# Attention scores as two products over 128 rows, with another order of the attention steps

## The chip, the cores and the metric

The kernel runs on one core of one Trainium2 chip. The engines of a core work side by side, each through its own queue in order: TensorE (PE, with its weight loads shown as PEld), VectorE (DVE), ScalarE (ACT), GpSimd (POOL), and SyncE (SP), which issues the DMAs. The metric is the device time of one run in microseconds; the lower the better.

## What is computed

The reference is one inference step of two trunk layers over 640 tokens of width 1024: 128 context tokens and 512 latent ones. A layer is an FFN, a mixer of four head groups (A, B, C, D), and a second FFN. The change lies in mixers A and B, which are attention with four query heads of width 64 over two key/value heads:

```python
q = rms_norm(q.reshape(B, T, n_kv, n_q // n_kv, HEAD_DIM), gq)
k = rms_norm(k.reshape(B, T, n_kv, HEAD_DIM), gk)
...
# B, dense, 128-query blocks; latent tokens read 256 cached and 512 own keys
s = jnp.einsum('bqkgd,bskd->bkgqs', qi, k).astype(jnp.float32) * scale
p = attn_probs(s, sink).astype(v.dtype)
return jnp.einsum('bkgqs,bskd->bqkgd', p, v)
...
# A, windowed: 256 cached keys and a band of up to 384 own keys, with a sink
s_band = jnp.einsum('bnqkgd,bnskd->bnkgqs', qb, kb).astype(jnp.float32) * scale
s_band = jnp.where(valid[None, :, None, None], s_band, NEG_INF)
s_ctx = jnp.einsum('bnqkgd,bckd->bnkgqc', qb, kc).astype(jnp.float32) * scale
```

Everything is float32. A context block (128 queries) reads only its own 128 keys.

## The kernel before

A float32 operand of a product is kept as two parts of a faster type (fp32r): `hi`, a rounded copy, and `lo`, the rest. A product of two such operands is three matmuls, hi·hi, hi·lo and lo·hi (`mm3`, lines 271 to 275, tiles `...h` and `...l`).

The mixer of a layer (`mixers`, from line 840 on) is written as Python generators, one for each strand of work, and each letter of the string `ORDER` (lines 40 to 42) runs one of them to its next `yield`: C and L the convolution and scan of mixer C, a, b, v, r, s mixer D, p and q the projections of A's and of B's queries, keys and values (`qkv`, a first step that takes the weights and five blocks of 128 tokens, twice), t and u their transposes (`qktr`), m and n the scores and softmax of A and of B, M and N the transposes of the probabilities and the products with the values behind them, c one half of an output chunk of the product of mixers C and D with the output weights (`down`, written `dn`), and "!" the load of the cached keys and values. At "|" PSUM is cut anew into two score tiles of two banks (`psS`) and four tiles of one bank (`psM`), which the projections (`nat`), transposes (`tr`, `pt`), products with values (`ao`) and `dn` share. A scheduler then sets the final order on each engine from this sequence, so neighbouring steps may be interleaved.

One step m or n is one head of one block of 128 queries, called a head here; there are 20 for A and 20 for B in each layer. Four of the 20 are the context block (128 keys), and the other 16 are long: 768 keys in B, 512 or 640 in A. TensorE makes its scores (`sc`) with the queries as the stationary operand. The head's 64 dimensions lie on 64 of the 128 partitions, the lower half for key/value head 0 and the upper for 1:

```python
r = slice(kv * 64, kv * 64 + 64)
qh, ql = qkh[g][r, b * 128:b * 128 + 128], qkl[g][r, b * 128:b * 128 + 128]
...
mm3(p[:, 256:512], qh, ql, ckh[r, ...], ckl[r, ...], True, True)
mm3(p[:, 512:512 + w], qh, ql, qkh[2][r, k0:k0 + w], qkl[2][r, k0:k0 + w], True, not band)
```

A band's edge is masked by one more matmul of 128 columns (line 1257). VectorE finds the maximum (`mx`, line 1264) and its negative (`nm`), ScalarE takes the exponential (`P`, line 1273), VectorE the reciprocal of the sum and the scaling of `P` (lines 1279, 1280). Then TensorE transposes `P` in pieces of 128 (line 1290), ScalarE copies them out (`PT`, 1291), TensorE multiplies with the values (1299), and ScalarE and VectorE split the result into parts (`mxh`, `mxl`, 1303, 1304). In a projection block ScalarE copies and squares (1173, 1174), VectorE and GpSimd normalise and rotate (1178 to 1201); `tr` (1154) transposes queries and keys with the tokens on columns and splits them (1160, 1161).

The weights come through a pool of 15 tiles (`wide`), shared with `P` and `PT`; ScalarE and VectorE split them (lines 168, 169).

Of the kernel before, what the change touches and what calls it, by code (L numbers as in the profile page):

```python
# [4 lines left out]
F32 = mybir.dt.float32  # L5
F32R = mybir.dt.float32r
# [19 lines left out]
HALF = ((320, 640), (0, 320))  # L26
EPS = 1e-6
# [13 lines left out]
    "CaCCCCvLvrLarvvvLLLbsLvpLrprbrssrqsrsrLsptrsLpppqLp|!sputpLsptcqpcmccpMmqMmmcqtMmMmmqmMMmmqMqMcmcqMm"  # L41
    "MuqmmqqccMMMmmmucMmMnnnuNcNNnnNnMNnnMNNmMncNncnnNNcnnNnNmnNNNMnNnNNnMccnMNNN",) * L
# [11 lines left out]
def trunk(tc, A, O):  # L54
# [3 lines left out]
    with ExitStack() as es:  # L58
# [7 lines left out]
        def banks(two, one):  # L66
            """PSUM as `two` tiles of two banks and `one` tiles of one"""
# [8 lines left out]
        def other():  # L76
            """the end of the stack of pools changes its form between the FFNs and the mixers"""
# [40 lines left out]
        # ---------------------------------------------------------------- constants, residual, conditions  # L118
# [18 lines left out]
        # ---------------------------------------------------------------- weights, prefetched in order  # L137
# [21 lines left out]
        def parts(src, n):  # L159
            """the two parts of a float32 operand"""  # L160
# [16 lines left out]
        def take(ahead=2, deep=0):  # L177
            """the next weights; those of the next `ahead` items are made, the next `deep` of them loaded"""
# [15 lines left out]
        def halved(ap, n):  # L194
            """a load of two items"""
# [5 lines left out]
        def seven(gate, up):  # L201
            """the weights of the seven products of one hidden chunk: gate = [A11 | A12], up = [A21 | A22]"""
# [68 lines left out]
        def mm3(out, wh, wl, xh, xl, first, last, more=False):  # L271
            """out (+)= w x, three products of their parts; `more` goes on with sums that were read already"""
# [11 lines left out]
        # ---------------------------------------------------------------- modulation  # L284
        # per (layer, group): tile [128, 2 conditions (latent, context), 8 chunks]
# [24 lines left out]
        def mod_row(l, g, k, c):  # L310
            """one condition's products for 128 columns of w_mod"""
# [19 lines left out]
        def after_start(n=""):  # L331
            """what is not needed at once issues behind the first norm"""
# [6 lines left out]
        def mod_load(k):  # L339
            """w_mod for the first norm's shift and scale, chunk k"""  # L340
# [7 lines left out]
        def mod_first(k):  # L348
            """shift and scale of the first norm, chunk k: eight products in four column groups, then their sum"""
# [49 lines left out]
        # ---------------------------------------------------------------- norm  # L399
# [437 lines left out]
        def mixers(l):  # L837
# [685 lines left out]
```

## Time and profile before

| | us |
|---|---|
| three runs | 2520.03, 2520.49, 2522.44 (median 2520.49) |
| profiled execution, span from its first to its last instruction | 2521.9 |
| first layer, last retention norm of D to the norm after the mixer | 637.1 to 837.0 |
| first score product, first and second layer | 656.8 and 1897 |
| last score product, first and second layer | 803 and 2041 |

The profile is of another execution than the three runs; its own time is known by its span alone, 1.4 us over the median of the runs. TensorE is busy for 98% of the span, VectorE for 78%, ScalarE for 45%. A matmul's shown length runs on past the start of the next, so a busy TensorE is not TensorE at its peak: what one product costs is read from start to start in the timeline. The two layers are alike, and the sections below read the first one.

### The profile page before, as it was taken

How to read it: one execution, taken by the hardware profiler on the slowest of the kernel's cores; microseconds unless marked ns; L12 is line 12 of the kernel's file. 1: busy time of each engine (PE TensorE's matmuls, PEld its weight loads, DVE VectorE, ACT ScalarE, POOL GpSimd, SP SyncE). 2: the span in 40 equal slices, each digit the busy share in tenths (PEclk: the TensorE clock that was granted, in tenths of full speed). 3: DMA queues.
4: the chain of work that ended last, by engine and by line, in shares of the span. 5: the costliest groups of instructions: out<-in, count | busy, mean ns of one | idle time of the engine just before them, and what ended most of it. 6: DMA issues, size and time to landing. Idle time of an engine off the chain costs nothing.

```text
span 2521.9 us, 43865 instructions
## 1 busy us (share of the span) xinstructions
PE 2467.4 (98%) x17376; PEld 2365.6 (94%) x17376; DVE 1974.8 (78%) x3850; ACT 1141.8 (45%) x2271; POOL 244.8 (10%) x251
## 2 busy tenths in 40 slices
PE   7999999999999999999999999999999999999999
PEld 6999999996888999999999999999878789999999
DVE  6899989856666898988989898897656668666765
ACT  5344334563345633443463344344634556433433
POOL 2100000022420200000020000000433102000000
PEclk9999999999999999999999999999999999999999
DMA  7544344222102244443424444342110022222222
GB/s 253 185 152 138 127 129 148 94 78 67 37 18 66 93 144 134 143 133 118 141 89 148 134 142 133 119 134 78 58 60 26 18 76 76 77 67 81 87 81 71
DMA packets 92303, 261.88 MB, mean 104 GB/s; under 512 B 10049, under 2 KB 20929, under 8 KB 92097
## 3 DMA queue, kind: packets, MB, share of 16 engines
q1 hardware_dynamic: 92096, 259.07, 31.7%
q8 instruction: 137, 2.24, 0.4%
q14 instruction: 70, 0.57, 0.1%
HBM read 255.63 MB, written 3.41 MB: 103 GB/s over the span
## 4 chain that ended last, share of the span: by engine, by line
PE 67%; DVE 4%; ACT 2%; POOL 1%; issue 1%; DVEq 0%; POOLq 0%; ACTq 0%
PE dn L273 8%; PE dn L274 7%; PE dn L275 7%; PE x L274 5%; PE x L275 5%; PE x L273 5%; PE y L274 3%; PE y L275 3%; PE y L273 3%; PE pt L1290 2%; PE ao L1299 2%; PE g L274 2%; PE g L273 2%; PE g L275 1%; PE z L273 1%; PE z L274 1%
## 5 line engine op out<-in xcount | busy, mean ns | idle before, releaser
L273 PE MATMUL dn<-hidh,wp 128*128 128x320 f32 x1408 | 434.5, 311 | 0.0
L275 PE MATMUL dn<-hidh,wp 128*128 128x320 f32 x1408 | 433.9, 309 | 0.0
L274 PE MATMUL dn<-hidl,wp 128*128 128x320 f32 x1408 | 433.7, 309 | 0.2 <-DVE hidl L281 0.2
L168 ACT ACTIVATE wp<-ws 128x512 fp32r<-128x512 f32 x288 | 180.8, 630 | 393.2 <-DVE ws L215 149.9
L168 ACT ACTIVATE wp<-raw 128x512 fp32r<-128x512 f32 (+1 forms) x408 | 243.7, 611 | 212.1 <-DVE wp L169 84.2
L682 DVE SCALAR_TENSOR_TENSOR x<-dn,mod,x 128x128 f32<-128x128 f32 (+3 forms) x488 | 233.8, 518 | 126.4 <-PE dn L275 125.3
L318 DVE SCALAR_TENSOR_TENSOR junk<-wm,cond 128x1024 bf16<-128x1024 f32 x256 | 304.5, 1218 | 4.6 <-DMA wm<-in_wmod 4.5
L169 DVE TENSOR_TENSOR wp<-raw,wp 128x512 fp32r<-128x512 f32 (+1 forms) x408 | 266.2, 667 | 51.9 <-ACT wp L168 47.0
L273 PEld LDWEIGHTS dn<-hidh,wp 128*128 128x128 f32 x1408 | 264.5, 188 | 4.8 <-ACT hidh L280 3.7
L274 PEld LDWEIGHTS dn<-hidl,wp 128*128 128x128 f32 x1408 | 264.8, 188 | 0.6 <-DVE hidl L281 0.6
L275 PEld LDWEIGHTS dn<-hidh,wp 128*128 128x128 f32 x1408 | 264.6, 188 | 0.0
L169 DVE TENSOR_TENSOR wp<-ws,wp 128x512 fp32r<-128x512 f32 x288 | 197.4, 691 | 17.6 <-ACT wp L168 17.0
L274 PE MATMUL g<-hl,whi 128*128 128x320 f32 x608 | 192.6, 318 | 3.2 <-DVE hl L528 1.7
L275 PE MATMUL g<-hh,wlo 128*128 128x320 f32 x608 | 190.5, 314 | 0.0
L273 PE MATMUL g<-hh,whi 128*128 128x320 f32 x608 | 185.5, 318 | 4.5 <-ACT hh L527 2.2
L273 PE MATMUL x<-hh,wp 128*128 128x320 f32 x576 | 178.3, 310 | 1.0 <-DVE sl L613 1.0
L274 PE MATMUL x<-hl,wp 128*128 128x320 f32 x576 | 178.5, 310 | 0.0
L275 PE MATMUL x<-hh,wp 128*128 128x320 f32 x576 | 178.3, 309 | 0.0
L169 DVE TENSOR_TENSOR wlo<-raw,whi 128x1024 fp32r<-128x1024 f32 x88 | 109.8, 1249 | 61.2 <-ACT whi L168 46.0
L425 POOL TENSOR_TENSOR nrs<-nrm,neghalf 80x4 f32<-80x4 f32 x12 | 13.3, 1106 | 1377.1 <-DVE nrm L423 1377.1
L168 ACT ACTIVATE whi<-raw 128x1024 fp32r<-128x1024 f32 x88 | 92.5, 1052 | 80.5 <-PE dk L274 20.7
L274 PEld LDWEIGHTS g<-hl,whi 128*128 128x128 f32 x608 | 117.1, 193 | 5.9 <-DVE hl L454 3.5
(331 smaller groups left out, 6655.2 us busy)
## 6 DMA issues: line engine op xcount, KB each, us to landing
raw<-in_wgu SPq DMA_DIRECT2D x176, 512.0 KB, 3.5
wm<-in_wmod SPq DMA_DIRECT2D x128, 512.0 KB, 4.0
raw<-in_wd SPq DMA_DIRECT2D x64, 512.0 KB, 3.8
raw<-in_wd SPq DMA_DIRECT2D x32, 384.0 KB, 3.4
raw<-in_wint SPq DMA_DIRECT2D x20, 512.0 KB, 3.5
wm<-in_wm SPq DMA_DIRECT2D x32, 256.0 KB, 5.5
raw<-in_wqkv SPq DMA_DIRECT2D x16, 512.0 KB, 3.5
raw<-in_wocd SPq DMA_DIRECT2D x8, 512.0 KB, 3.4
```

The lines of the kernel that those rows point to most:

```text
L168: S.activation(hi, src, AF.Copy)
L169: V.tensor_sub(lo, src, hi.bitcast(F32))
L273: PE.matmul(out, wh, xh, start=first, stop=False, skip_group_check=more)
L274: PE.matmul(out, wh, xl, start=False, stop=False, skip_group_check=more)
L275: mark["pe"] = PE.matmul(out, wl, xh, start=False, stop=last, skip_group_check=more)
L318: V.scalar_tensor_tensor(junk, modraw["w"], 1.0, cond[c], OP.mult, OP.mult, accum_out=modraw[(l, g)][:, c, k:k + 1])
L425: G.tensor_tensor(r, s, neghalf[:80, :4], op=OP.pow)
L682: V.scalar_tensor_tensor(x[d][:, s0:s1], pv[:, s0 - base:s1 - base], gate[:, c, d:d + 1], x[d][:, s0:s1], OP.mult, OP.add)
L1290: PE.transpose(p[:, c0 - a0:c0 - a0 + 128], P[:, c0:c0 + 128], idn)
L1299: PE.matmul(o[kv * 64:kv * 64 + 64, :128], vs[i][:, kv * 64:kv * 64 + 64], pts[kv][:, i * 128:i * 128 + 128], start=i == 0, stop=i == nb - 1)
```

## The change

Queries are no longer kept as a hi tile and a lo tile with two key/value heads on the two halves of the partitions. For each key/value head there is one tile `q2` of all 128 partitions: hi on the 64 rows of that head, lo on the other 64. Keys are doubled: a tile `kkh` (hi) and a tile `kkl` (lo) for each key/value head hold the same 64 rows twice. A product of `q2` with `kkh` over 128 rows is hi·hi + lo·hi, and one with `kkl` is hi·lo + lo·lo. So `mm2` makes two matmuls where `mm3` made three. To double the keys, the last addition of the key projection writes them twice (`qq`, 256 columns in place of 128), and the transposes of keys take two pieces in place of one. The copies and splits out of PSUM are made per 64 rows for queries. The cached keys are loaded with two DMAs for each key/value head and split per head, in `wide` tiles. `ORDER` is new after "|": "!" stands behind the projections, right ahead of the first m; eight of the twelve steps q come before the first m (three before); c steps are spread, five before the first n (ten before) and eleven behind. The rest of the diff takes comments out.

```diff
+ROWS = (slice(0, 64), slice(64, 128))
 ORDER = (
-    "...Lp|!sputpLsptcqpcmccpMmqMmmcqtMmMmmqmMMmmqMqMcmcqMm"
-    "MuqmmqqccMMMmmmucMmMnnnuNcNNnnNnMNnnMNNmMncNncnnNNcnnNnNmnNNNMnNnNNnMccnMNNN",) * L
+    "...Lp|spqtpqLsptqpqpqtq!mqmmqMmqMmMmqMmMmuMmcMmuMmMmcM"
+    "mMmuMmcMmuMmMmcMmMmcMnMnMMncNnNncNnNncNnNncNnNncNnNnNncNnNncNnNncNnNnNNcNcNc",) * L
...
                 def tr(tiles, blocks, chunks):
-                    for i_, c in enumerate(chunks):
+                    t0, n = blocks[0] * 128, len(blocks) * 128
+                    c = slice(t0, t0 + n)
+                    if len(chunks) == 1 and not ks:
+                        ks.extend((slot("kkh", F32R, T), slot("kkl", F32R, T)) for _ in ROWS)
+                    if len(chunks) == 2 and not qs:
+                        qs.extend([slot("q2", F32R, T) for _ in ROWS] for _ in range(2))
+                    for i_ in range(2):
                         p = psM("tr")
-                        t0, n = blocks[0] * 128, len(blocks) * 128
                         for i, b in enumerate(blocks):
                             PE.transpose(p[:, i * 128:i * 128 + 128], tiles[b][:, i_ * 128:i_ * 128 + 128], idn)
-                        S.activation(qk[0][c][:, t0:t0 + n], p[:, :n], AF.Copy)
-                        V.tensor_sub(qk[1][c][:, t0:t0 + n], p[:, :n], qk[0][c][:, t0:t0 + n].bitcast(F32))
+                        if len(chunks) == 1:
+                            hi, lo = ks[i_]
+                            S.activation(hi[:, c], p[:, :n], AF.Copy)
+                            V.tensor_sub(lo[:, c], p[:, :n], hi[:, c].bitcast(F32))
+                        else:
+                            for kv in range(2):
+                                t, r, o = qs[i_][kv], ROWS[kv], ROWS[1 - kv]
+                                S.activation(t[r, c], p[r, :n], AF.Copy)
+                                V.tensor_sub(t[o, c], p[r, :n], t[r, c].bitcast(F32))
...
+                        if pas == 0:
+                            twice = thin("qq", 256)
...
+                            if b == 0:
+                                S.activation(out, q4, AF.Copy)
+                            else:
+                                V.tensor_add(out, q4, r4)
+                            q = twice
...
             def load_cache():
-                ck = slot("ck", F32, 512)
-                D.dma_start(out=ck, in_=A["ck"][l])
+                cache["k"] = []
+                for kv in range(2):
+                    ck = wide("ck", 512)
+                    for r in ROWS:
+                        D.dma_start(out=ck[r], in_=A["ck"][l][ROWS[kv]])
+                    cache["k"].append(parts(ck, 512))
...
                 def scores(b, g, kv):
-                    r = slice(kv * 64, kv * 64 + 64)
-                    qh, ql = qkh[g][r, b * 128:b * 128 + 128], qkl[g][r, b * 128:b * 128 + 128]
+                    q2 = qs[g][kv][:, b * 128:b * 128 + 128]
+
+                    def mm2(out, keys, c, last=True):
+                        PE.matmul(out, q2, keys[0][:, c], start=True, stop=False)
+                        PE.matmul(out, q2, keys[1][:, c], start=False, stop=last)
...
-                        mm3(p[:, 256:512], qh, ql, ckh[r, m * 256:m * 256 + 256], ckl[r, m * 256:m * 256 + 256], True, True)
+                        mm2(p[:, 256:512], cache["k"][kv], slice(m * 256, m * 256 + 256))
...
-                        mm3(p[:, 512:512 + w], qh, ql, qkh[2][r, k0:k0 + w], qkl[2][r, k0:k0 + w], True, not band)
+                        mm2(p[:, 512:512 + w], ks[kv], slice(k0, k0 + w), not band)
```

Three places in the built order show what moves, all in the first layer. Line numbers of the changed kernel differ from those of the kernel before.

On TensorE, a head of B with the transposes around it, before:

```order
L1290 MATMUL pt<-idn,P 128x128 x3
L273 MATMUL sc<-ckh,qkh 128x256
L274 MATMUL sc<-ckl,qkh 128x256
L275 MATMUL sc<-ckh,qkl 128x256
L273 MATMUL sc<-qkh 128x512
L274 MATMUL sc<-qkl,qkh 128x512
L275 MATMUL sc<-qkh,qkl 128x512
L1290 MATMUL pt<-idn,P 128x128 x9
```

and now (the cached keys' parts are called `wp`):

```order
L1323 MATMUL pt<-idn,P 128x128 x6
L1271 MATMUL sc<-wp,q_8001 128x256
L1272 MATMUL sc<-wp,q_8001 128x256
L1271 MATMUL sc<-kkh,q_8001 128x512
L1272 MATMUL sc<-kkl,q_8001 128x512
L1323 MATMUL pt<-idn,P 128x128 x6
L1332 MATMUL ao<-PT,cv 64x128 x4
```

Six score products have become four, and each pair of `ao` products over both heads stands between heads as it did.

On VectorE, among the long heads of A, before (`q`, `r`, `qss` are the projection blocks of step q):

```order
L1178 TENSOR_REDUCE qss<-qsq 128x4
L1179 TENSOR_SCALAR qss<-qss 128x4
L1183 TENSOR_TENSOR q<-q,qrr 128x256
L1277 TENSOR_TENSOR sum<-sum,esink 128x1
L1197 TENSOR_TENSOR r<-q,rsin 128x8x16 x2
L1279 RECIPROCAL rc<-sum 128x1
L1280 TENSOR_SCALAR P<-P,rc 128x640
L1201 TENSOR_TENSOR q<-q,r 128x256
L1161 TENSOR_TENSOR qkl<-tr,qkh 128x512
L1264 TENSOR_REDUCE mx<-sc 128x1
L1178 TENSOR_REDUCE qss<-qsq 128x4
L1268 TENSOR_SCALAR nm<-mx,negsink 128x1
```

and now:

```order
L1313 TENSOR_SCALAR P<-P,rc 128x640
L1337 TENSOR_TENSOR mxl<-ao,mxh 128x128
L1297 TENSOR_REDUCE mx<-sc 128x1
L1301 TENSOR_SCALAR nm<-mx,negsink 128x1
L1169 TENSOR_TENSOR kkl<-tr,kkh 128x512 x2
L1297 TENSOR_REDUCE mx<-sc 128x1
L170 TENSOR_TENSOR wlo<-raw,whi 128x1024
L1301 TENSOR_SCALAR nm<-mx,negsink 128x1
L170 TENSOR_TENSOR wlo<-raw,whi 128x1024
L1310 TENSOR_TENSOR sum<-sum,esink 128x1
L1312 RECIPROCAL rc<-sum 128x1
L1313 TENSOR_SCALAR P<-P,rc 128x640
```

The projection blocks have gone from between the heads (they stand ahead of the first head); the splits of doubled keys of B and of output weights stand there now.

On ScalarE, the split of the cached keys (`ckh` before, `wp<-ck` now), before:

```order
L168 ACTIVATE whi<-raw 128x1024
L1119 ACTIVATE so<-st 64x256
L280 ACTIVATE ckh<-ck 128x512
L1173 ACTIVATE q<-nat 128x256
L1174 ACTIVATE qsq<-nat 128x256
L1160 ACTIVATE qkh<-tr 128x128
L1160 ACTIVATE qkh<-tr 128x512
```

and now:

```order
L1186 ACTIVATE q<-nat 128x256
L1187 ACTIVATE qsq<-nat 128x256
L169 ACTIVATE wp<-ck 128x512
L1186 ACTIVATE q<-nat 128x128
L1187 ACTIVATE qsq<-nat 128x128
L1189 ACTIVATE vn<-nat 128x128
L169 ACTIVATE wp<-ck 128x512
L1186 ACTIVATE q<-nat 128x256
L1187 ACTIVATE qsq<-nat 128x256
L1173 ACTIVATE q_7115<-tr 64x512
```

It has moved down in the queue, in between the copies that empty the last projection tiles ahead of the first head, and there are two of it.

## Rows read from the trace of the kernel before

**Rows 1.** The page, busy time of each engine (share of the span), instructions

```profile
...
PE 2467.4 (98%) x17376; PEld 2365.6 (94%) x17376; DVE 1974.8 (78%) x3850; ACT 1141.8 (45%) x2271; POOL 244.8 (10%) x251
...
```

**Rows 2.** Windows, first layer: us, busy PE, PEld, DVE, ACT, POOL, PEclk, DMA

```profile
...
677.80:741.50 63.70, 60.81 (x469) 52.34 (x466) 41.64 (x128) 30.91 (x91) 16.55 (x20) 0.95 0.08 26
...
747.20:803.00 55.80, 55.19 (x462) 44.18 (x461) 37.03 (x93) 34.09 (x88) 0.00 (x0) 1.00 0.06 20
...
sum 200.00, PE 192.81 PEld 168.79 DVE 128.63 ACT 97.67 POOL 37.55; mean PE 32.14 PEld 28.13 DVE 21.44 ACT 16.28 POOL 6.26
```

**Rows 3.** The same windows, instructions that write or read the scores alone

```profile
...
677.80:741.50 63.70, 19.97 (x108) 12.19 (x86) 10.72 (x14) 11.75 (x28) 0.95 0.08 26
...
747.20:803.00 55.80, 21.43 (x110) 14.17 (x109) 15.90 (x18) 16.79 (x36) 1.00 0.06 20
...
sum 200.00, PE 45.11 PEld 28.77 DVE 29.55 ACT 32.74; mean PE 7.52 PEld 4.80 DVE 4.93 ACT 5.46
```

**Rows 4.** Timeline, TensorE, one head: start us, us, instruction

```profile
...
765.06 0.38 PE L273 MATMUL sc<-ckh,qkh 64*128 64x256 f32 x1
765.29 0.28 PE L274 MATMUL sc<-ckl,qkh 64*128 64x256 f32 x1
...
765.53 0.39 PE L273 MATMUL sc<-qkh 64*128 64x512 f32 x1
...
765.99 0.39 PE L275 MATMUL sc<-qkh,qkl 64*128 64x512 f32 x1
766.31 0.42 PE L273 MATMUL dn<-mxh,whi 128*128 128x320 f32 x1
766.56 0.31 PE L274 MATMUL dn<-mxl,whi 128*128 128x320 f32 x1
```

**Rows 5.** Timeline, TensorE, two heads queued together

```profile
...
768.26 0.38 PE L273 MATMUL sc<-ckh,qkh 64*128 64x256 f32 x1
...
768.72 0.38 PE L273 MATMUL sc<-ckh,qkh 64*128 64x256 f32 x1
768.72 0.39 PE L273 MATMUL sc<-qkh 64*128 64x512 f32 x1
...
769.64 0.39 PE L275 MATMUL sc<-qkh,qkl 64*128 64x512 f32 x1
```

**Rows 6.** Timeline, TensorE, 128-row products of 256 columns, and a wait

```profile
...
667.55 0.28 PE L1026 MATMUL nat<-whi,hl 128*128 128x256 f32 x1
667.67 0.28 PE L1027 MATMUL nat<-wlo,hh 128*128 128x256 f32 x1
669.45 0.30 PE L1290 MATMUL pt<-idn,P 128*128 128x128 f32 x1 [1.51 <-DVE P L1280]
```

**Rows 7.** Timeline, TensorE, five transposes and the longest wait

```profile
...
721.56 0.71 PE L1290 MATMUL pt<-idn,P 128*128 128x128 f32 x5
724.76 0.51 PE L1299 MATMUL ao<-PT,cv 128*64 128x128 f32 x5 [2.49 <-DVE x L682]
```

**Rows 8.** Windows, two stretches of lower TensorE clock, columns as above

```profile
...
671.40:674.70 3.30, 3.30 (x16) 3.30 (x15) 2.65 (x13) 2.17 (x7) 0.83 (x2) 0.50 0.00 0
726.00:732.70 6.70, 6.42 (x37) 5.46 (x36) 2.85 (x7) 2.18 (x6) 2.28 (x2) 0.50 0.00 0
```

**Rows 9.** Lines by form, VectorE, 677.8 to 741.5: busy us, mean ns | idle

```profile
...
L1264 DVE TENSOR_REDUCE mx<-sc 128x1 f32<-128x640 f32 x8 | 6.6, 824 | 4.8 <-PE sc L1257 4.8
...
L169 DVE TENSOR_TENSOR wlo<-raw,whi 128x1024 fp32r<-128x1024 f32 x3 | 3.7, 1217 | 0.0
...
L1183 DVE TENSOR_TENSOR q<-q,qrr 128x256 f32<-128x256 f32 x5 | 2.1, 426 | 3.8 <-POOL qrr L1181 3.8
...
L1161 DVE TENSOR_TENSOR qkl<-tr,qkh 128x512 fp32r<-128x512 f32 x3 | 2.0, 685 | 0.4 <-ACT qkh L1160 0.4
...
```

**Rows 10.** One tile, the cached keys' load

```profile
...
DMA to landing us min/median/max: 3.8/4.0/4.1
```

More of the change, by code (lines that the diff above doesn't have):

```diff
@@ L1149, in qkv @@
                 vn = slot("vn", F32, T)
-                qk = [slot("qkh", F32R, T) for _ in range(3)], [slot("qkl", F32R, T) for _ in range(3)]
-                att[m] = (qk, vn)
+                qs, ks = [], []
+                att[m] = (qs, ks, vn)
                 ready = trs.setdefault(m, [])
                 def tr(tiles, blocks, chunks):
-                    for i_, c in enumerate(chunks):
+                    t0, n = blocks[0] * 128, len(blocks) * 128
[5 more added lines that the diff above has]
+                    for i_ in range(2):
                         p = psM("tr")
-                        t0, n = blocks[0] * 128, len(blocks) * 128
                         for i, b in enumerate(blocks):
                             PE.transpose(p[:, i * 128:i * 128 + 128], tiles[b][:, i_ * 128:i_ * 128 + 128], idn)
-                        S.activation(qk[0][c][:, t0:t0 + n], p[:, :n], AF.Copy)
-                        V.tensor_sub(qk[1][c][:, t0:t0 + n], p[:, :n], qk[0][c][:, t0:t0 + n].bitcast(F32))
+                        if len(chunks) == 1:
[7 more added lines that the diff above has]
+                                V.tensor_sub(t[o, c], p[r, :n], t[r, c].bitcast(F32))
                 for pas in range(2):
@@ L1200, in qkv @@
                             G.tensor_mul(q3, q3, cs)
-                            V.tensor_add(q[:, :nw], q[:, :nw], r[:, :nw])
+                            if pas == 1:
+                                V.tensor_add(q, q, r)
+                        if pas == 0:
+                            twice = thin("qq", 256)
+                            q4, r4 = (t[:, :128].rearrange("p (h d) -> p h d", h=2)[:, :, None, :].to_broadcast([128, 2, 2, 64])
+                                      for t in (q, q if b == 0 else r))
+                            out = twice.rearrange("p (h c d) -> p h c d", h=2, c=2)
+                            if b == 0:
[3 more added lines that the diff above has]
+                            q = twice
                         tiles[b] = q
@@ L1219, in load_cache @@
             def load_cache():
-                ck = slot("ck", F32, 512)
-                D.dma_start(out=ck, in_=A["ck"][l])
+                cache["k"] = []
[4 more added lines that the diff above has]
+                    cache["k"].append(parts(ck, 512))
                 cv = slot("cv", F32, 512)
                 D.dma_start(out=cv, in_=A["cv"][l])
-                cache["k"], cache["v"] = split(ck, "ck", 512), cv
+                cache["v"] = cv
             def attention(m):
-                (qkh, qkl), vn = att[m]
-                (ckh, ckl), cv = cache["k"], cache["v"]
+                qs, ks, vn = att[m]
+                cv = cache["v"]
                 for g in range(2):
```

4 lines of the change are left out of this document (2 added, 2 removed).

## Prediction

> **What bounds the kernel now.** I read the page first: TensorE is busy for 98% of the span and VectorE for 78% [rows 1], so TensorE is the engine to look at. Then the windows over 200 us of the first layer, from the last projections to the norm behind the mixer. The two windows that matter are A's long heads (677.8 to 741.5, with projection blocks of B between them) and B's (747.2 to 803). TensorE fills 60.8 of 63.7 us in the one and 55.2 of 55.8 in the other, VectorE 41.6 and 37.0 [rows 2]. So in both stretches the end is set by what TensorE is given, and the other engines have a third to spare. The same windows for the scores alone say how much of that the change touches: 45.1 us of TensorE in the layer, 20.0 in A's window and 21.4 in B's [rows 3]. Last the timeline, where the reader should look at starts and not at lengths. A head of B alone takes its six products from 765.06 to 766.31, 1.25 us: 0.23 for the first product of 256 columns although the second to follow it needs 0.12, 0.23 for each of 512, and 0.32 for the last until the next work starts, whose own first product then takes 0.25 [rows 4]. So going into 64-row products and out of them costs about 0.3 us a head, beside the columns. Products over 128 rows follow each other without that: 256 columns each 0.12 [rows 6], that is 0.47 ns a column.
>
> **The scores, cost by cost.** Two products over 128 rows replace three over 64. No product of 128 rows and 512 columns of this type stands in the trace. Scaled from 256 columns it takes 0.24; the nearest row, 64 rows and 512 columns, has 0.23 [rows 4]. I take 0.24. It can hardly be less; if 128 rows streamed at half that rate, it would be 0.48. Then a long head of B is 2 x 0.12 + 2 x 0.24 = 0.72, against 1.25 and the 0.1 that the next product loses: 0.6 less. Not every head stands alone, though. At 768.72 products of two heads, one on each half of the rows, start at the same time, and two heads take from 768.26 to 0.32 behind 769.64, 1.70 [rows 4, 5], against 1.44 with the change. There the gain is only 0.13 to 0.18 a head.
>
> So the sum is made from the total, in which overlap is counted once. Before: 45.1 [rows 3], less 0.07 for each of 40 heads, by which a last length of 0.39 passes the next start at 0.32: 42.3. After, by columns: A has eight heads of 512 keys and eight of 640, 2 x 9216 = 18,432 columns or 8.7 us; B has 16 of 768, 24,576 columns or 11.6; the eight context heads have 16 products of 128 columns, 1.9 if each took as long as one of 256; 24 mask products of 128 columns stay, 1.4. Together 23.6, so 18.7 less, and up to 3 us more where the work behind a head no longer starts with a slow product. I take 19 a layer. If the 512 columns took 0.48, 32 x 0.24 = 7.7 of it would go.
>
> **What is added.** Transposes of keys: ten more pieces a layer. Five take 0.71 with one latency of 0.30 in it [rows 6, 7], so 0.10 each: +1.0 on TensorE. On VectorE and ScalarE each split of queries becomes two of 64 rows, and one split of keys becomes two. A split of 512 columns takes 0.69 [rows 9], and if 64 rows take as long as 128, that is six more splits of 512 and six of 128 columns (0.3 each, by the same row) a layer and engine, 6 us of VectorE, spread over 200 us in which it has 71 to spare [rows 2]. The doubled last addition of the keys adds less than 0.2 for each of eight blocks. These are hidden over the layer as a whole; whether they are hidden where they fall is the next point.
>
> **What is moved.** Five projection blocks leave A's window for the time ahead of the first head. TensorE's work in A's window becomes 60.8 - 20.0 + 10.9 (scores, 8.7 with masks and tails) - 14.4 (five blocks of 24 products at 0.12) + 3.2 (some 24 transposes and a dozen `ao` that fall inside the stretch now, 0.06 to 0.10 each) = 40.5 us. VectorE's stretch in the built order has 118 instructions where 128 stand in the window; at 41.6/128 = 0.325 each that is 38.4, and some 40 since splits replace short steps. So there the cover is gone: both engines have 40 us, and each hand-over between them (scores, maximum, exponential, scaling, transposes) can stop TensorE. It waited 2.9 us in this window before and 0.6 in B's [rows 2]. I take 3 more in A's and 1 more in B's, where TensorE keeps the lead: 55.2 - 21.4 + 11 = 45 and more `dn`, against VectorE's 37 and what those bring. Bounds: 0, if the `dn` blocks fill every wait, to 14, at 0.45 for each of 32 long heads (a wait for one `P` was 1.51 [rows 6], so a third of that every time).
>
> The projection blocks cost the same ahead of the heads as between them; with GpSimd they make a chain of their own there, which two strands, p and q, hide.
>
> The load of the cached keys is moved too. Its DMAs stand behind two weight loads on SP's queue, and the second head's pair waits there for a projection's last product to free its tile; the output-weight loads queue behind it and are not needed for several microseconds. On ScalarE the split stands in front of the copies that free projection tiles, and a load takes 4.0 to land [rows 10]. So copies can be late by 4 us while TensorE has two blocks (48 x 0.12 = 5.8 us) to do and four one-bank tiles for them. Bounds 0 and 4 a layer; I take 0.5, since the blocks nearly cover it.
>
> **The sum.** A layer: -19 + 1 + 4 + 0.5 = -13.5. Two layers: -27. From the profiled span: 2521.9 - 27 = 2494.9. The runs' median lies 1.4 below that span, so 2493.5, say **2494**, with a range of its own of 2483 to 2506.
>
> **Rivals.** *Full gain.* The `dn` blocks, now spread evenly among the heads, take up all waits, and the old ones go as well: 2.49 where TensorE waited for a PSUM tile behind `dn` [rows 7], 1.51 for a `P` [rows 6], and half of the 10 us a layer that it spent at a granted clock of 0.50 behind them [rows 8]. For it: VectorE is at 64% over the 200 us [rows 2]. Against: A's window is even at 40 to 40. A layer -18 - 4 - 3 = -25, or -22 if the low clock stays: 2470 to 2476.
>
> *The balance eats it.* Both windows pay 0.45 a head, 14 a layer, and the load of keys 2 more: -18 + 16 = -2 a layer, 2516. For it: two score tiles let TensorE run only two heads ahead. Against: in B's window TensorE waited 0.6 us in all.
>
> *Slower, by the clock.* Behind two waits TensorE ran at a granted clock of 0.50, 1.2 GHz of its 2.4, for 3.3 and 6.7 us, in which it did 16 and 37 products [rows 8]. If the many short waits of A's and B's windows do the same, each microsecond of its 85 us of work there costs one more. It decides from 23.5 us of such work in a layer on: the 13.5 gained and 10 of slack that waits and the old low clock make up. At half of the work, 42 less 23.5, it is +18.5 a layer: about 2557; a third gives 2530. For it: the low stretches begin behind waits. Against: in B's window the clock was 1.00 with VectorE hand-overs between all heads [rows 2]. The page "TensorE: Matmul & The Clock Gate" of the Trainium skill (Part 1, "HAM oscillation") says that frequent idling between bursts of matmuls can bring the clock down repeatedly; the trace shows it for single long waits only.
>
> *Slower, by lost overlap.* Products on the two halves of the rows can run at once, as [rows 5] shows at 768.72, and 128-row products cannot. If all pairs of heads of the kernel before did so without a loss, a pair in B would cost 3 x 0.36 = 1.08 and now 1.44, in A about 0.8 and 1.07: 8 x 0.36 + 8 x 0.27 = 5 more a layer, with transposes and waits 2 x 10 in all, about 2540. Against it: the pair that did overlap took 1.70, and 45.1 us [rows 3] is twice the 22 that such overlap throughout would give. The same page of the Trainium skill (Part 3, "Packing small matmuls") has the rule: products in different row groups run concurrently, which by itself speaks for leaving the 64 rows as they are; the trace shows it in part.
>
> *It does not do what it says*: 512 columns over 128 rows at 0.48. Then -5.8 a layer, 2509; inside the range.
>
> **Chances.** The forecast with the 0.48 case 0.60, full gain 0.16, balance 0.13, clock 0.07, lost overlap 0.04. The range of 8 in 10 reaches from the full gain to the balance case: **2470 to 2518**. What a measurement of this kernel tells from no change is about 0.2%, 5 us: 2515.5 to 2525.5 is the same. Faster 0.60 + 0.16 + 0.04 (the better part of balance) = 0.80, the same 0.09, slower 0.11.
>
> **What the changed profile would show.** Scores per layer near 25 us of TensorE in place of 45.1, no slow first and last product in a head, starts 0.12 and 0.24 apart: if 512 columns stand at 0.4 or more, the price was wrong. A's long heads in some 45 us with TensorE and VectorE both near 40; if TensorE waits over 10 us there, the balance case holds. Granted clock at 1.00 in B's stretch; below 0.9 in either, the clock case. A wait of a projection behind the split of the cached keys of under 1 us. The forecast is wrong if the layers shrink by under 7 or over 20 us, or if time changes outside the mixers.

## The result, and the profile after

The changed kernel takes 2537.35 us (median of 4 runs, 2536.34 to 2538.78), the kernel before 2521.47 beside it: a ratio of 1.0055, 95% interval 1.0039 to 1.0072. It is slower by 14 us; the forecast was faster by 27, and the range did not hold the time. The profiled execution spans 2537.0 us. The kernel before itself ranges from 2519 to 2533 us over the runs beside the experiments, its mean granted clock from 0.994 to 0.986, so small differences are read from the ratios and their intervals and not from single times.

TensorE has less work and the span is longer. The page of the changed kernel, which answers to [rows 1]:

```profile
PE 2448.2 (96%) x17252; PEld 2363.3 (93%) x17252; DVE 1986.8 (78%) x3876; ACT 1149.7 (45%) x2301; POOL 238.8 (9%) x251
```

The windows of the first layer say where (columns as in [rows 2]): up to the first heads in two pieces, context heads, A's long heads, B's, and what follows the last score.

```profile
639.20:656.00 16.80, 16.06 (x145) 15.55 (x144) 9.21 (x26) 4.09 (x14) 11.06 (x13) 1.00 0.15 40
656.00:685.00 29.00, 18.82 (x125) 18.21 (x126) 14.78 (x43) 8.43 (x25) 12.11 (x17) 0.82 0.04 10
685.00:697.90 12.90, 11.90 (x97) 11.06 (x96) 8.48 (x37) 4.95 (x21) 6.68 (x8) 1.00 0.00 1
697.90:754.00 56.10, 46.31 (x354) 39.32 (x352) 40.86 (x120) 33.31 (x100) 4.92 (x6) 0.85 0.09 29
754.00:803.70 49.70, 48.40 (x416) 42.56 (x416) 37.99 (x101) 31.23 (x83) 0.00 (x0) 1.00 0.07 23
803.70:844.10 40.40, 39.46 (x325) 38.37 (x326) 23.95 (x42) 20.22 (x33) 0.00 (x0) 1.00 0.35 117
sum 204.90, PE 180.95 PEld 165.06 DVE 135.26 ACT 102.24 POOL 34.77; mean PE 30.16 PEld 27.51 DVE 22.54 ACT 17.04 POOL 5.80
```

Before, the time up to A's long heads had two windows:

```profile
637.10:656.80 19.70, 18.05 (x153) 17.13 (x151) 12.65 (x30) 5.71 (x17) 13.86 (x13) 1.00 0.08 21
656.80:677.80 21.00, 19.27 (x136) 18.13 (x135) 12.99 (x50) 6.37 (x25) 7.13 (x11) 0.92 0.08 27
```

TensorE idles 10.2 of 29.0 us ahead of the first head and 9.8 of 56.1 among A's long heads, and in both windows its granted clock is below 1.00. Up to A's long heads 58.7 us pass where 40.7 passed. By estimate 45.7 would have done: 130 more projection products (`nat`) stand there at 0.12 us, and 60 `dn` products of 10.6 us have gone. So some 13 us are lost there. B's window is as quiet as before and 6 us shorter, which the tail gives back: 211 `dn` products stand behind the last score where 175 stood. The whole mixer of the first layer is 204.9 us, against 199.9 from 637.1 to 837.0 before.

The scores themselves do what was asked of them. One head of B (timeline of TensorE, against [rows 4]) and the sum for the scores alone, against [rows 3]:

```profile
774.86 0.39 PE L1271 MATMUL sc<-wp,q 128*128 128x256 f32 x1
775.08 0.28 PE L1272 MATMUL sc<-wp,q 128*128 128x256 f32 x1
775.20 0.39 PE L1271 MATMUL sc<-kkh,q 128*128 128x512 f32 x1
775.43 0.40 PE L1272 MATMUL sc<-kkl,q 128*128 128x512 f32 x1
775.66 0.82 PE L1323 MATMUL pt<-idn,P 128*128 128x128 f32 x6
...
sum 204.90, PE 36.30 PEld 21.84 DVE 29.50 ACT 32.96; mean PE 6.05 PEld 3.64 DVE 4.92 ACT 5.49
```

From start to start 0.22, 0.12, 0.23, 0.23: 0.80 us a head where it was 1.25. A product of 512 columns costs 0.23 over 128 rows as over 64. The sum of 36.3 is made of shown lengths, which run past the next start, and some of A's scores stand at half the clock (below).

**Ahead of the first head.** The waits of TensorE between 639 and 686 us (engine, line, what it waited for: us in total, times, longest):

```profile
PE tr L1165 <- DVE q L1215: 8.0, 2, 4.9
PE nat L1026 <- ACT qsq L1187: 2.9, 1, 2.9
```

The longest is for a block's rotated queries. VectorE's timeline in that stretch shows why; the bracket at the end of a row is the idle time ahead of it and what ended it:

```profile
667.46 0.17 DVE L1192 TENSOR_SCALAR qss<-qss 128x4 f32<-128x4 f32 x1
668.75 0.43 DVE L1196 TENSOR_TENSOR q<-q,qrr 128x256 f32<-128x256 f32 x1 [1.12 <-POOL qrr L1194]
669.10 0.68 DVE L170 TENSOR_TENSOR wp<-ck,wp 128x512 fp32r<-128x512 f32 x1
670.39 0.50 DVE L1210 TENSOR_TENSOR r<-q,rsin 128x128 f32<-128x128 f32 x2 [0.62 <-POOL q L1198]
670.80 0.28 DVE L1191 TENSOR_REDUCE qss<-qsq 128x2 f32<-128x128 f32 x1
671.79 0.42 DVE L1215 TENSOR_TENSOR q<-q,r 128x256 f32<-128x256 f32 x1 [0.71 <-POOL q L1213]
672.14 0.16 DVE L1192 TENSOR_SCALAR qss<-qss 128x2 f32<-128x2 f32 x1
673.11 0.29 DVE L1196 TENSOR_TENSOR q<-q,qrr 128x128 f32<-128x128 f32 x1 [0.81 <-POOL qrr L1194]
```

A block goes three times to GpSimd and back, and VectorE stands idle each time; the next block's steps come behind. From `qss` to `qss` this block takes 4.7 us (667.46 to 672.14), and four blocks in a row 4.3 on the mean (659.08 to 676.42), while the 24 products of one take TensorE 2.9 (24 x 0.12). The 60 `dn` products that stood ahead of the long heads before, 24 of them ahead of the first head, are gone from there too: nothing fills the difference.

The wait of 2.9 us is of another kind. The `qsq` that empties a projection tile stands on ScalarE behind D's last split, which waits for a GpSimd step of 1.6 us:

```profile
656.80 0.74 ACT L281 ACTIVATE mxh<-ro 128x640 fp32r<-128x640 f32 x1 [8.21 <-POOL ro L1137]
```

**Among A's long heads.** The longest wait there is 3.15 us at 717.8, for a copy of transposed probabilities. Timelines of TensorE, VectorE, then ScalarE:

```profile
720.94 0.33 PE L1323 MATMUL pt<-idn,P 128*128 128x128 f32 x1 [3.15 <-ACT PT L1324]
```

```profile
717.22 0.81 DVE L1297 TENSOR_REDUCE mx<-sc 128x1 f32<-128x640 f32 x1
717.95 1.22 DVE L170 TENSOR_TENSOR wlo<-raw,whi 128x1024 fp32r<-128x1024 f32 x1
719.08 0.21 DVE L1301 TENSOR_SCALAR nm<-mx,negsink 128x1 f32<-128x1 f32 x1
```

```profile
719.38 0.29 ACT L1309 ACTIVATE esink<-sink,nm 128x1 f32<-128x1 f32 x1 [1.79 <-DVE nm L1301]
719.58 1.04 ACT L169 ACTIVATE whi<-raw 128x1024 fp32r<-128x1024 f32 x1
720.53 0.64 ACT L1324 ACTIVATE PT<-pt 128x256 f32<-128x256 f32 x2
```

The head's `nm` has to wait behind a split of output weights on VectorE, ScalarE's queue stands behind that `nm`, then makes another split, and only then comes the copy that TensorE wants. VectorE is idle for 27% of this window and ScalarE for 41%; this wait comes from what stands in front.

**The clock.** Windows over the four slow stretches of the layer; before it had the two of [rows 8]:

```profile
670.00:677.25 7.25, 4.98 (x24) 4.98 (x25) 3.37 (x12) 0.99 (x3) 3.28 (x6) 0.53 0.01 2
680.25:684.00 3.75, 3.10 (x15) 3.10 (x16) 2.33 (x5) 2.57 (x6) 0.13 (x1) 0.54 0.00 0
700.75:711.25 10.50, 8.32 (x35) 6.76 (x36) 7.87 (x29) 6.14 (x23) 3.51 (x5) 0.51 0.24 80
721.25:728.25 7.00, 6.60 (x37) 5.57 (x35) 3.71 (x10) 4.01 (x12) 0.00 (x0) 0.51 0.01 4
```

28.5 us in all at or near 1.2 GHz of 2.4, each stretch in or behind a wait of 2.3 us or more.

**The loss in three parts.** TensorE's idle time follows from the page: 2537.0 less 2448.2 is 88.8 us, where 2521.9 less 2467.4 was 54.5 [rows 1]. All stretches of the whole execution at a granted clock of 0.50, added up, before and now:

```profile
sum 38.13, PE 34.68 PEld 29.05 DVE 27.39 ACT 17.07 POOL 12.89; mean PE 3.47 PEld 2.90 DVE 2.74 ACT 1.71 POOL 1.29
sum 75.10, PE 65.93 PEld 57.94 DVE 52.18 ACT 34.09 POOL 17.56; mean PE 4.40 PEld 3.86 DVE 3.48 ACT 2.27 POOL 1.17
```

Half of TensorE's busy time in them counts as lost (a product of 384 columns takes 0.32 us from start to start there, 0.17 at 1.00): 17.3 us before, 33.0 now. So idle time is up by 34.3 us and the low clock takes 15.6 more, while the work that is left, counted at the full clock, is down by 34.9, 17.4 a layer. The change took the work away that it was meant to take; the waits and the clock behind them took more than that back.

### The profile page after: what moved, and what is told of

Its sections match the earlier page's. It is cut to its first block, busy times and chain, and to the rows that moved or that the text cites. A ratio compares the mean times of both kernels' runs of the same rounds, so it can differ in the third digit from the quotient of the medians.

```text
span 2537.0 us, 43717 instructions
## 1 busy us (share of the span) xinstructions
PE 2448.2 (96%) x17252; PEld 2363.3 (93%) x17252; DVE 1986.8 (78%) x3876; ACT 1149.7 (45%) x2301; POOL 238.8 (9%) x251
## 5 line engine op out<-in xcount | busy, mean ns | idle before, releaser
L170 DVE TENSOR_TENSOR wp<-ws,wp 128x512 fp32r<-128x512 f32 x288 | 197.9, 692 | 17.3 <-ACT wp L169 16.8
L1026 PE MATMUL nat<-whi,hh 128*128 128x256 f32 x400 | 119.5, 299 | 9.2 <-ACT qsq L1187 5.8
L169 ACT ACTIVATE whi<-raw 128x1024 fp32r<-128x1024 f32 x88 | 92.6, 1052 | 66.3 <-DVE pmc L1092 13.7
```

The costliest lines, as they stand in the source:

```text
L169: S.activation(hi, src, AF.Copy)
L170: V.tensor_sub(lo, src, hi.bitcast(F32))
L1026: PE.matmul(p[:, :n], hh[:, t0:t0 + 128], wh[:, w0:w0 + n], start=k == 0, stop=False)
```

## The experiments

Theory 1 after the result: the order loses what the scores gain. Theory 2: shorter scores make the waits wherever they stand. Ratios are to runs of the kernel before that were taken beside the run; microseconds that are worked out from ratios are of 2521.

**Scores and order apart.** The kernel before with the new ORDER alone:

```diff
-ORDER = ("...|!sputpLsptcqpcmccpMmqMmmcqt...
+ORDER = ("...|spqtpqLsptqpqpqtq!mqmmqMmqMmMm...
```

> The kernel before (three products of 64 rows) with the new ORDER alone. Theory 1, the order loses what the scores gain: the projection chain ahead of the first head leaves TensorE 9 us more of waits and 3 to 7 us more of low clock in a layer, and of the 8 us of new waits among A's heads about half remain, since each head's scores are 0.6 us longer. That is +14 to +18 a layer, 2550 to 2558 us. Theory 2, the shorter scores themselves make the waits (a head gives TensorE too little work to cover VectorE's softmax): with long scores the waits are gone, 2521 to 2528 us.

2561.83 us, ratio 1.0157 (1.0140 to 1.0174). The order costs 40 us with the old operands, somewhat more than theory 1 said; it was right in kind.

**Other orders of the changed kernel**, three runs. First, c ahead of the heads:

```diff
-|spqtpqLsptqpqpqtq!mq...  nNncNnNncNnNnc...
+|spqtpqLsptqcpqcpqctq!mq...  nNnNnNncNnNn...
```

> The changed kernel with three of the sixteen c steps (half chunks of the output product, about 3.4 us of TensorE each) taken out of B's part and put among the projection blocks ahead of the first head, where TensorE waited 2.9, 4.9 and 3.1 us in the first layer. Theory 1: about 8 us of these waits go and with them 3 us of low clock, B's part gives back up to 3: 2515 to 2524 us. Theory 2: the waits only move behind the heads, 2534 to 2540 us.

2532.24, 1.0036 (1.0022 to 1.0050): better by 5 us (the intervals still overlap), not by 13 to 22. TensorE still waited 9.7 us ahead of the first head (3.8 for rotated queries, 2.9 and 1.1 for steps of blocks, 1.9 for VectorE's `x` of the c steps): filler that needs VectorE itself stands in the same queue.

```diff
+|spqtpqLsptqppt!mmqmMmMqmMmMqmMmMqmMmMqmMmMqmMmMqmMumMuc...
```

> The changed kernel with B's last five projection blocks put back among A's heads, c steps in number as in the changed kernel (five in A's part, eleven behind). Theory 1: TensorE has 14 us of projections to fill A's hand-overs, and fewer blocks wait ahead of the first head: waits fall from 26 to about 12 us a layer and low clock from 7 to 3: 2500 to 2515 us. Theory 2 (the shorter scores make the waits, VectorE bounds A): the projection blocks bring VectorE 2 us each into A's part, no gain, 2530 to 2545 us.

2571.33, 1.0193 (1.0177 to 1.0209): a miss for theory 1. Its waits lie among the heads (5.9 us for a block's queries, among the context heads, and five of 1.5 to 2.9 for exponentials).

```diff
+|spqtpqLsptqcpqcpqctq!mmqmMmMqcmMmMqcmMmMqcmMmMcmMmMucm...
```

> The changed kernel with three c steps among the projections ahead of the first head, eight (in place of five) among A's heads, and the last four projection blocks of B among them too; five c steps left for B's part. Theory 1: both places of the new waits are filled; waits near the 9 us a layer of the kernel before, low clock 3 to 4 us: 2490 to 2505 us, faster than both kernels. Theory 2: 2530 us or more, since VectorE bounds A and B then stands without cover.

2551.24, 1.0115 (1.0096 to 1.0135): a miss too. So these three placings of filler do not mend it, and the last two lists may differ from the tuned one in more than what they were made for; why each is that slow is not settled.

**The whole old ORDER under the new scores**, with pools to hold it:

```diff
-NSLOT = 41, NTHIN = 14, ORDER new
+NSLOT = 42, NTHIN = 11, ORDER of before
```

> The two-product scores with the whole ORDER of the kernel before, '!' at its old place. The doubled keys need one work tile more than the old order leaves, so the work pool has 42 tiles (41) and the pool of thin tiles 11 (14). Theory 1, the order alone loses: scores give back 17 us a layer, and the waits stay near the 9 us of the kernel before, plus 2 to 5 where the shorter heads no longer cover a hand-over: 2490 to 2502 us. Theory 3 (from the runs so far: shorter scores bring waits wherever VectorE's softmax is not covered): half of the 17 is given back, 2504 to 2515 us.

2554.92, 1.0112 (1.0098 to 1.0127): both theories miss. The scores lose in the old order too. One place, on VectorE, 3.5 us of TensorE's wait for a context head's `P`:

```profile
666.68 0.21 DVE L1302 TENSOR_SCALAR nm<-mx,negsink 128x1 f32<-128x1 f32 x1
667.35 0.43 DVE L1216 TENSOR_TENSOR q<-q,r 128x256 f32<-128x256 f32 x1 [0.46 <-POOL q L1214]
667.69 1.13 DVE L684 SCALAR_TENSOR_TENSOR x<-dn,mod,x 128x320 f32<-128x320 f32 x3
668.74 1.21 DVE L171 TENSOR_TENSOR wlo<-raw,whi 128x1024 fp32r<-128x1024 f32 x1
669.87 0.15 DVE L1311 TENSOR_TENSOR sum<-sum,esink 128x1 f32<-128x1 f32 x1
...
670.32 0.28 DVE L1314 TENSOR_SCALAR P<-P,rc 128x128 f32<-128x128 f32 x1
```

The head's sum and scaling stand behind 2.3 us of other work (`x`, `wlo`): 3.6 us from its `nm` to the scaling. With the old operands and the same pools (the run after next) it is 1.7 us, 661.32 to 663.05. This place alone does not price the preparation: the run with halved queries below keeps the wait of 3.5 us and is 24 us faster.

With the load late (`sptcqpc!m` for `|!s`):

> As the run with the old ORDER and new scores, but '!' (load of the cached keys and values) stands right ahead of the first m as in the changed kernel. Theory 1: the place of the load decides little, 0 to 4 us over that run. Rival: a load that lands 4 us after its issue and is split behind projection copies holds back the first long heads, 6 to 12 us over it.

2558.77, 1.0120 (1.0101 to 1.0140), not to be told from 1.0112: in this order the place of the load decides little.

The pools alone (kernel before, 42 and 11):

> The kernel before with the pools of that run alone (42 work tiles, 11 thin ones), scores and ORDER as before. All theories: the pools alone do nothing, 2518 to 2526 us; if three thin tiles fewer hold projections back, 2530 and more, and the run with new scores is read against this one.

2527.03, 1.0007 (0.9996 to 1.0019): nothing.

**Preparation and products apart.** All operands as changed, three products of 64 rows:

```diff
-PE.matmul(out, q2, keys[0][:, c], start=True, stop=False)
-PE.matmul(out, q2, keys[1][:, c], start=False, stop=last)
+PE.matmul(out, qh, keys[0][r, c], start=True, stop=False)
+PE.matmul(out, qh, keys[1][r, c], start=False, stop=False)
+PE.matmul(out, qh, keys[0][r, c], start=False, stop=last)
...
```

In the old ORDER:

> As the run of the new scores with the old ORDER (2554.9 us; pools of 42 and 11), all preparation as changed (stacked queries, doubled keys, split cached keys), but each score again as three products of 64 rows from these tiles (the third takes the high part of the queries for the low one, so the numbers are off; the work is that of the kernel before). Theory A, the preparation is what loses in the old order (ten more transposes, some 10 us more of VectorE and 5 of ScalarE a layer, in front of waiting heads): at 17 us a layer more of TensorE no faster, 2555 to 2580 us. Theory B, the shorter scores lose the cover that TensorE's own time gave VectorE's softmax: the waits go down by what the products go up, and it stands at 2530 to 2550 us, faster than with the short scores.

2578.01, 1.0214 (1.0198 to 1.0230). In the new one:

> The changed kernel (new ORDER, stacked queries, doubled keys) with each score again as three products of 64 rows (the third takes the high part of the queries for the low one, so the numbers are off). With the runs so far it closes a square: against the changed kernel (2537.4) it gives the worth of the shorter scores in the new order, against the old scores in the new ORDER (2561.8) the price of the preparation there. Theory A, the preparation loses where it falls among heads (old order, +51 us for two layers) and is hidden ahead of them (new order): 2558 to 2566 us. Theory B, it costs as much in either order: 2580 us or more.

2569.61, 1.0173 (1.0151 to 1.0195). This closes the square (us over the kernel before, ratio less 1 times 2521):

| | old operands, three products | new operands, three products | new operands, two products |
|---|---|---|---|
| old ORDER | +2 (pools) | +54 | +28 |
| new ORDER | +40 | +44 | +14 |

Read across: two products for three give 26 us in the old order and 30 in the new, 13 to 15 a layer. Preparing the operands costs 52 in the old order, and 4 in the new, where the intervals overlap. Theory A of these runs holds.

Read down: with the old operands the new order is 38 us worse, and with the new ones 10 to 14 better. So neither the order nor the preparation has a price of its own. Together, still with three products, they cost 44 us, 22 a layer.

The square also judges theory 2. From the first long head to the last score of the first layer, in the new order with three products and with two, then in the old order the same:

```profile
695.70:821.30 125.60, 119.43 (x867) 96.68 (x866) 83.61 (x225) 67.34 (x186) 6.40 (x9) 0.90 0.07 22
693.60:803.70 110.10, 99.01 (x801) 85.71 (x801) 80.88 (x226) 65.91 (x189) 7.24 (x9) 0.92 0.08 25
684.20:833.40 149.20, 135.53 (x971) 110.09 (x969) 89.71 (x246) 73.13 (x200) 15.54 (x20) 0.89 0.05 16
683.70:818.60 134.90, 116.57 (x901) 99.84 (x903) 87.39 (x244) 71.58 (x198) 14.55 (x18) 0.90 0.05 17
```

TensorE's busy time falls by 20 and 19 us, and its idle time rises by 5 in either order (6.2 to 11.1, 13.7 to 18.3). Shorter scores do bring waits, but they cost a quarter of what the scores save.

**Which preparation.** In the old ORDER one piece at a time is halved, made for one key/value head and used for both (three runs, with one of the three edits each; the loops that fill the tiles are shortened with them):

```diff
-qs.extend([slot("q2", F32R, T) for _ in ROWS] for _ in range(2))
+qs.extend([slot("q2", F32R, T)] * 2 for _ in range(2))
-ks.extend((slot("kkh", F32R, T), slot("kkl", F32R, T)) for _ in ROWS)
+ks.extend([(slot("kkh", F32R, T), slot("kkl", F32R, T))] * 2)
-for kv in range(2):
+for kv in range(1):          # load_cache
...
```

> The run of the new scores with the old ORDER (2554.9 us), but the stacked queries are made for the first key/value head alone and used for both (half of the 64-row splits of queries, 8 copies and 8 subtractions a layer fewer, 4 us of VectorE; numbers are off). If the splits of the queries are what the preparation costs, 2530 to 2542 us; if not, 2550 to 2556 us.

2530.13, 1.0018 (1.0007 to 1.0029).

> The same run with doubled keys made for the first key/value head alone and used for both (half of the transposes and splits of keys: 10 transposes, 4 copies and 4 subtractions a layer fewer, 2 us of VectorE; numbers are off). If the keys' second piece is what costs, 2530 to 2542 us; if not, 2550 to 2556 us.

2537.82, 1.0047 (1.0030 to 1.0065).

> The same run with the cached keys loaded and split for the first key/value head alone and used for both (two DMAs, one copy and one subtraction a layer fewer, and one of the 15 wide tiles free through the attention; numbers are off). If the wide tile that the second head's parts hold takes weights' room and so delays the output weights' splits into the heads, 2530 to 2545 us; if not, 2550 to 2556 us.

2539.54, 1.0050 (1.0032 to 1.0067). Against 1.0112 each takes 16 to 24 us away, together more than the whole loss of 28. No single piece is guilty, and the pieces do not add up: each of the three expectations came true by its number, and together they can't all be the cause. Between the profiled executions most of it is the clock. The loss at 0.50, counted as above, is 35.8 us with all pieces and 19.5, 22.8 and 22.8 with one halved; TensorE's idle time falls less, from 93.5 to 83.8, 89.0 and 90.8. What in a piece does it is not shown: a piece takes 4, 2 or 0.7 us of VectorE a layer and some of ScalarE, it holds tiles of the pools (the wide tile of the last expectation among them), and the scheduler sets another order for each of these kernels.

**The softmax's own length.** The changed kernel without VectorE's scaling of `P`:

```diff
-V.tensor_scalar(P[:, :w], P[:, :w], rc, None, OP.mult)
```

> The changed kernel without the scaling of P by the reciprocal of its sum (VectorE, 40 steps of 0.3 to 0.7 us a layer; the probabilities stay unnormalised). Theory B, A's and B's windows are bounded by the hand-over score, maximum, exponential, scaling, transposes: about 0.6 us a head off the chain and 20 us a layer off VectorE; most of the 10 us of waits in A and B and the low clock behind them go: 2508 to 2522 us. Theory A or a loss ahead of the heads alone: what waits in A and B waits for other things, 2528 to 2538 us.

2530.44, 1.0024 (1.0014 to 1.0034): 8 us for some 20 us a layer of VectorE taken away. The load of VectorE alone does not bound A and B.

**The chain of a block.** GpSimd's two products go to VectorE:

```diff
-G.tensor_mul(q[:, :nw], q[:, :nw], gain[:, g0:g0 + nw])
+V.tensor_mul(q[:, :nw], q[:, :nw], gain[:, g0:g0 + nw])
-G.tensor_mul(q3, q3, cs)
+V.tensor_mul(q3, q3, cs)
```

> The changed kernel with the two GpSimd products of each projection block (by the gain, by the cosines; 0.74 us each and about 0.6 us idle on VectorE at each hand-over) on VectorE (about 0.43 us each, no hand-over). If the chain of a block between VectorE and GpSimd sets the time ahead of the first head (4.4 us a block where TensorE needs 2.9), a block goes to about 3 us: nine blocks by 1.2 us, less what the later heads lose to a busier VectorE: 2515 to 2528 us. If it does not: 2536 to 2545 us.

2521.67, 0.9991 (0.9982 to 0.9999): 16 us off, as much as the change had lost, with more work on VectorE. Between the profiled executions TensorE's idle time gives 5 of it (88.8 to 83.4) and the low clock 11 (33.0 to 22.0).

> The same move of the two GpSimd products to VectorE in the kernel before. There most blocks stand among heads and few waits were for them (1.0 and 0.6 us in the first layer): no gain ahead of the heads, some more load on VectorE in A's window, 2520 to 2535 us. If that chain is hidden in both, the two runs move alike.

2514.41, 0.9962 (0.9950 to 0.9975): 10 us in the kernel before, where no gain was expected. TensorE's idle time falls by 2 us only (54.5 to 52.4), and the low clock gives 7 (17.3 to 10.6): both stretches of [rows 8] are gone.

```profile
637.00:677.00 40.00, 37.99 (x311) 36.02 (x309) 29.87 (x96) 12.56 (x44) 10.29 (x10) 1.00 0.07 21
677.00:741.00 64.00, 61.45 (x492) 53.05 (x492) 47.38 (x159) 33.42 (x100) 6.60 (x7) 1.00 0.08 26
```

So 10 of the 16 us in the changed kernel are not the change's own, and against this kernel it is still 7 us slower.

Then the second half of a block behind the first half of the next:

```diff
+def rest(b=b, q=q, rr=rr):
+    ...            # normalise, rotate
+late.append(rest)
+while late and (b in (0, 4) or len(late) > 1):
+    late.pop(0)()
```

> The changed kernel with the two GpSimd products on VectorE as in the run of 2521.7 us, and in addition each projection block's second half (normalise, rotate) written behind the first half (copies, squares, sum) of the next block, so that VectorE has another block's work while GpSimd takes the inverse root (1.0 us, VectorE idle 1.1 to 1.2). If the serial chain of blocks still sets the time ahead of the first head (TensorE waited 1.7, 3.8 and 2.1 us there in the first layer), 3 to 5 us a layer go: 2510 to 2517 us. If what is left there waits for other things, 2518 to 2526 us.

2514.10, 0.9959 (0.9946 to 0.9972): 8 us more. TensorE's waits from 639 to 686 us, 10.9 in the changed kernel and 7.8 with the first edit, are 5.0 now, nearly all of it one wait for rotated queries that is as long as the longest was:

```profile
PE tr L1165 <- DVE q L1217: 4.8, 1, 4.8
```

> The same two edits in the kernel before (with the first edit alone 2514.4 us). Its blocks stand mostly among heads, where VectorE has other work during GpSimd's root: little more to gain, 2510 to 2518 us.

2519.21, 0.9976 (0.9963 to 0.9989): in the kernel before it gains nothing over the first edit alone, rather loses; a little outside what was expected.

These two runs say what the chain cost the change. The two edits take 24 us from the changed kernel and 6 from the kernel before; the difference, 18, is as much as the 14 that the change lost, or more. With both edits in both kernels the changed one is 4 us ahead (0.9959 against 0.9976), and the intervals overlap.

> The changed kernel with both edits and three c steps among the projections ahead of the first head (which alone gave 5 us). Whichever cover the serial chain lacked, both together should leave little of the wait ahead of the first head: 2500 to 2512 us, faster than both kernels; if the c steps only bring their weights' splits in front of the chain, no better than without, 2512 to 2520 us.

2510.46, 0.9945 (0.9928 to 0.9961), the fastest median, faster than both kernels; from the kernel before with the first edit (0.9962) its interval does not part it. Waits of TensorE from 639 to 686 us, now with the first heads in that stretch, and the windows ahead of the long heads and over A's:

```profile
PE tr L1166 <- DVE q L1218: 2.7, 2, 1.8
PE sc L1277 <- ACT P L1312: 1.6, 1, 1.6
```

```profile
637.10:679.00 41.90, 39.20 (x330) 38.21 (x329) 31.69 (x93) 14.54 (x42) 12.57 (x12) 1.00 0.11 36
679.00:742.00 63.00, 51.88 (x434) 45.84 (x433) 50.73 (x162) 37.74 (x121) 5.30 (x5) 0.95 0.06 18
```

The clock is 1.00 up to A's long heads (0.91 from 639.2 to 697.9 in the changed kernel). From the first long head to the last score TensorE still idles 11.7 us, against 11.1 in the changed kernel and 3.8 in the kernel before; in the runs with two products whose ORDER keeps A's part as it was, it is 9 to 12, and none has removed it.

## Why the prediction was wrong

**The price of the products: right.** 0.24 was taken for 512 columns, 0.23 measured; a head of B 0.72 against 0.80, since the first product still loses 0.1 (so this part of the 0.3 a head was no cost of 64 rows). The gain was put at 18 a layer net of transposes, and TensorE's work fell by 17.4. The waits that short scores bring were put at 4 and are 5, so that the square gives 13 to 15 a layer, where the prediction had 15 for the two together. The sign that it named for this, scores near 25 us, was missed (36.3 by shown lengths, some at half the clock).

**The added load: right in size, wrong in price.** VectorE was to get 6 us more a layer and has 6.6 (135.3 against 128.6 in [rows 2]). "Spread over 200 us in which it has 71 to spare" was the wrong question. In the old order preparing the operands costs 26 us a layer, in the new one at most a few: free engine time does not decide it. That a head's small steps stand behind the added ones in an engine's queue is what the rows above suggest; no run shows it by itself.

**The step that failed: "The projection blocks cost the same ahead of the heads as between them; with GpSimd they make a chain of their own there, which two strands, p and q, hide."** Two strands do not hide it, since VectorE takes one block's steps after the other's: 4.3 to 4.7 us a block where TensorE has 2.9. It waited 10.9 us there in the first layer, 8.0 of it for blocks, against 1.0 for a block and 0.6 for D's last split before, and the `dn` products that stood beside them had left. The row for it was in the trace: [rows 9] has 3.8 us of VectorE's idle time ahead of five `q`, ended by `qrr`. The step put the move at nothing, and the prediction put the clock at nothing as well; what it had for all that is new beside the products and their waits was 1.5 us a layer, and the square has 22. Shortening the chain gave 16 us, overlapping it 8 more, 18 in all beyond what the same edits gave in the kernel before.

**A's window: the term was mis-sized.** Both engines were put at 40 us, and VectorE has 40.9. The hand-overs were put at 3 us more; TensorE idles 9.8 us there against 2.9, and the low clock, put at nothing, takes 7.5 (half of the busy time in two of the four stretches) against 3.2 [rows 8]. The order quoted ahead of the prediction shows where the longest wait comes from: two `wlo` on either side of a head's `nm`. I counted those rows and did not read what waits behind them.

**B's window, the load of keys: right.** TensorE idles 1.3 us in B, and the load's place costs nothing that can be told (measured in the old order).

**The rivals.** What came is "the balance eats it" with the clock's rival added to it, but for the larger part in a place that neither named: each priced the heads alone and took what stands ahead of them as unchanged. By the prediction's own sign, a clock below 0.9 in A's stretch, it is the clock's rival, which had 7 in 100. Lost overlap is out: two products gain in both orders. Waits bring the granted clock down again and again here, in four stretches of 28.5 us in all in the first layer, though B's waits of 0.2 to 0.8 us left it at 1.00. The page "TensorE: Matmul & The Clock Gate" of the Trainium skill (Part 1, "HAM oscillation") describes matmuls that start again at the low clock after each long wait between bursts. The trace agrees with it in these four stretches.

## What to carry to other kernels

Where TensorE is busy for 98%, price not only the work that is taken from it but the chain that remains (its hops, in the order in which the queues will take them); the free time of the other engines is no price. Before moving a chain of small steps away from the work that covered it, measure its period alone (here 4.3 to 4.7 us a block for 2.9 of products); shortening it gave back as much as the change had lost, and helped the kernel before too. Count what a wait costs in the granted clock behind it: here that was about a third of all that was lost. An edit's gain in the changed kernel says little until the same edit has been made in the kernel before. In a built order, read for each short step of a hand-over what long step stands directly in front of it.

## What was not expected of the hardware

A long wait is paid twice: in or behind four of the layer's five longest the granted clock was near 0.50, in windows of 3.75 to 10.5 us. A step on GpSimd costs VectorE more than the same step of its own: a product of 0.72 us left VectorE idle for 0.71 although another step of 0.28 stood in between, where the product takes 0.43 on VectorE itself; and the inverse root of four columns, 1.01 us, left it idle for 1.12. A split of 64 rows takes as long as one of 128 (0.685 against 0.687 us for 512 columns).
